# Making twenty gate tiles in pairs with seven half-size products each

## The chip, the cores and the metric

The kernel runs on one core of a Trainium2 chip. The metric is the time of one execution on the device, in microseconds (us). The kernel before takes 2025.02 us (median of three runs, 2023.78 to 2026.5).

Engines are named as the profile names them. PE is the matrix engine: in `matmul(o, w, x)` the second argument is the stationary 128 x 128 operand, the third the moving one, whose columns stream through. PEld is its weight load, which overlaps the matmul. DVE is the vector engine, ACT the scalar (activation) engine, POOL is GpSimd. SP issues DMAs. SBUF is the on-chip working memory and PSUM the memory that matmuls write to, in banks of 512 floats per partition.

## The reference

One layer of a decoder trunk is applied to 2048 prompt positions and to 8 x 8 sample positions. What matters here is the gated merge of three branches:

```python
xn = _rmsnorm(x, p["norm_w"])
h = jnp.einsum("btd,de->bte", xn, p["w_in"])
q, k, v, z_a, gate_b, gate_c, h_b, z_b, u, v_c, z_c, g = _split_cols(h)
...
gates = jax.nn.sigmoid(g + p["b_gate"]).reshape(n, t, N_BRANCHES, D_MODEL)
...
a = jnp.einsum("bte,ed->btd", jax.nn.silu(z_a) * y_a, p["w_out_a"])
b = jnp.einsum("bte,ed->btd", jax.nn.silu(z_b) * y_b, p["w_out_b"])
c = jnp.einsum("bte,ed->btd", jax.nn.silu(z_c) * y_c, p["w_out_c"])
m = gates[:, :, 0] * a + gates[:, :, 1] * b + gates[:, :, 2] * c
return x + jnp.einsum("btd,de->bte", m, p["w_o"])
```

The width is 1024, so `g` has 3072 columns: 24 tiles of 128 columns, each a product of a 1024 x 128 weight with xn. Branches have 512 channels.

## The kernel before

Positions are taken in four blocks (`SBS`): three of 512 positions, and a last one of 576 (512 prompt positions and the 64 sample positions), which is worked in two chunks of 288 columns. Every block goes through the same phases: keys and values, queries, attention (mixed into the next phases), the convolution branch, the chunk branch, the gate phase and the output phase.

All data is float32, and a product is made with two parts of each operand: `split` (L170 and L171) makes the high part by an ACT cast to the format that PE multiplies, and the low part by a DVE subtraction. `gemm_t` then issues three matmuls for each 128 rows of the contraction, high x high, high x low and low x high (L179, L180, L181). The normalised x stands in SBUF as `xh` and `xl`, eight tiles of 128 rows.

Weights come one unit after another in the order that `order()` lists. `load_to` brings a unit by DMA into one of three `raw` tiles (a `wt` unit, that is one gate tile, has 1024 columns, 512 KB), `split_to` splits it into one of four `wh`/`wl` pairs, and `take` hands it to the matmuls. Splits are issued two units ahead of their use, and a load is issued as soon as a raw tile is free. The SP queue works its DMAs in program order, and a DMA that waits for a free tile holds back those behind it. PE and SP follow the program's order. The order of the other engines is set by a scheduler when the program is built; each of these queues is worked in order too.

The gate phase (`gate_phase`) runs over d = 0..7 (128 channels of the model width) and b = 0..2 (the branches). Gate tile j = 3d + b takes 24 matmuls (8 contraction tiles x 3) into one PSUM tile `ps_mm`, of which there are three; ACT applies the sigmoid with its bias (L773) into `t`. Then 12 matmuls make the branch's projection with a `wout` unit (512 columns), DVE multiplies it by the gate (L789) and adds the three branches up (L793). After the third branch the sum is split into `mh` and `ml`, the operands of the output phase. The squares of the next block's x, for its norm, are made in this phase from a tile of their own.

PSUM further holds two `ps_tp` banks for transposes and the banks `S0`, `S1` and `pv`, one tile each, which attention uses; in the gate phase they are idle.

Of the kernel before, what the change touches and what calls it, by code (L numbers as in the profile page):

```python
# [16 lines left out]
P = 128  # L17
# [32 lines left out]
def trunk_kernel(ctx: ExitStack, tc: tile.TileContext, A, O):  # L50
# [9 lines left out]
    def ps_mm():  # L60
        return psum.tile([P, 512], F32, tag="mm", name="ps_mm", bufs=3)
# [36 lines left out]
    def order():  # L98
        for _ in SBS:
            for j in range(6):  # L100
                yield "wn", j
            for j in range(28):
                yield "wt", j
            for j in range(6, 10):
                yield "wn", j
            for j in range(24):
                yield "wt", 28 + j
                yield "wout", j
            for j in range(KT):
                yield "wo", j  # L110

    units = [(n, j, A[n][j]) for n, j in order()]
    loaded, ready, taken = [], [], [0]
    ahead = dict(loads=0, splits=0)

    def load_to(j):
        while len(loaded) < min(j, len(units)):
            src = units[len(loaded)][2]
            raw = raws.tile([P, WE], F32, tag="raw", name="raw")
            nc.sync.dma_start(raw[:, : src.shape[1]], src)  # L120
            loaded.append(raw)

    def split_to(j):
        while len(ready) < min(j, len(units)):
            i = len(ready)
            load_to(i + 1)
            n = units[i][2].shape[1]
            wh = wts.tile([P, WE], F32R, tag="wh", name="wh")
            wl = wts.tile([P, WE], F32R, tag="wl", name="wl")
            split(wh[:, :n], wl[:, :n], loaded[i][:, :n])  # L130
            loaded[i] = None
            ready.append((wh, wl))
            load_to(i + 1 + ahead["loads"])

    def take(name, j):
        i = taken[0]
        assert units[i][:2] == (name, j), (units[i][:2], name, j)
# [58 lines left out]
    def xrstd(sb):  # L196

        t0, _, chunks, _ = SBS[sb]
        n = chunks[-1][1]
        tiles = [(c, min(c + P, n)) for c in range(0, n, P)]  # L200
        st = {"x": res.tile([P, 4 * TMAX], F32, tag="za", name="xbuf")}
        st["r"] = res.tile([P, TMAX], F32, tag="acc", name="acc")[:, :n]
        r = small.tile([P, 8], F32, tag="xr", name="xr")

        def piece(j, c0, c1):
            w = c1 - c0
            x = st["x"][:w, j % 2 * D:(j % 2 + 1) * D]
            nc.sync.dma_start(x, A["xn"][t0 * P + c0:t0 * P + c1])
            nc.scalar.activation(x, x, AF.Square, accum_out=r[:w, j:j + 1])

        def fin():
            for j0, j1, w in ((0, n // P, P), (n // P, len(tiles), n % P)):
                if w and j1 > j0:
                    rstd(r[:w, j0:j1], r[:w, j0:j1], j1 - j0, D)

        def spread():
            for t in (tiles[:4], tiles[4:]):
                if t:
                    ps = ps_tp()
                    b = t[0][0]  # L220
                    for c0, c1 in t:
                        w = c1 - c0
                        nc.tensor.transpose(
                            ps[:, c0 - b:c1 - b], r[:w, c0 // P:c0 // P + 1].broadcast_to([w, P]), ident[:w, :w]
                        )
                    nc.scalar.copy(st["r"][:, b:t[-1][1]], ps[:, : t[-1][1] - b])

        return st, [lambda j=j, c=c: piece(j, *c) for j, c in enumerate(tiles)] + [fin, spread]

    def xsplit(sb, st):  # L230
        t0, _, chunks, _ = SBS[sb]
        n = chunks[-1][1]

        def load(k):
# [12 lines left out]

        return [lambda k=k: piece(k) for k in range(KT)]
# [438 lines left out]
    def chunk_phase(sb, br, samp_args):  # L687
# [12 lines left out]
        br2 = [res.tile([P, 4, TMAX], F32R, tag="br2" + x, name="br2" + x) for x in "hl"]  # L700
        br.append(br2)
        vbuf = res.tile([P, 4 * 1024], F32R, tag="mh", name="vbuf")
        if sample:
            pair_sample("ml")
        def mixed(i, rows, t, gg):

            ts = slice(i * P, i * P + rows)
# [18 lines left out]
        def spatial(i, vh, vl, t, gg):  # L726
# [8 lines left out]
            if gg.stop == 4:  # L735
                mixed(i, P, t, slice(0, 4))

        for i, o, rows in wide(6, wide_outs(ntile, sample)):
            ssq = small.tile([P, 1], F32, tag="vssq", name="vssq")
            vn = tmp("vn", [P, 512])  # L740
            nc.scalar.activation(vn[:rows], o, AF.Square, accum_out=ssq[:rows])
            r = small.tile([P, 1], F32, tag="vr", name="vr")
            rstd(r[:rows], ssq[:rows], 1, 512)
            nc.vector.scalar_tensor_tensor(vn[:rows], o, r[:rows], vnw[:rows], ALU.mult, ALU.mult)
            if i == ntile:
                nc.sync.dma_start(O["scv"], vn[:rows])
                later(AT_SPATIAL + SPATIAL_AFTER * i, lambda vn=vn: spatial_sample(vn))
            else:
                v0 = i * 1024
                vh, vl = vbuf[:, v0:v0 + 512], vbuf[:, v0 + 512:v0 + 1024]  # L750
                split(vh, vl, vn)
                t = side("sp", [P, 4, P])
                for j in range(2):
                    gg = slice(2 * j, 2 * j + 2)
                    later(AT_SPATIAL + SPATIAL_AFTER * i + SPATIAL_EVERY * j, lambda a=(i, vh, vl, t, gg): spatial(*a))

    def keep(new, old):

        tc.keep_in_program_order(nc.scalar.dma_start(O[new][:, : P - TS, :], A[old][:, TS:, :]))

    def gate_phase(sb, br):
        chunks = SBS[sb][2]
        n = chunks[-1][1]
        m = None
        for d in range(KT):
            acc = None
            for b in range(3):
                wg = take("wt", 28 + 3 * d + b)
                t = tmp("t", [P, n])
                for c0, c1 in chunks:  # L770
                    pg = ps_mm()
                    gemm_t(pg, wg, KT, *xr, c0, c1)
                    nc.scalar.activation(t[:, c0:c1], pg[:, : c1 - c0], AF.Sigmoid, bias=bg[:, 8 * b + d:8 * b + d + 1])  # L773
                if d == 0 and b == 2:
                    flush()
                    m = [res.tile([P, KT, TMAX], F32R, tag="m" + x, name="m" + x) for x in "hl"]
                    if sb + 1 < len(SBS):
                        st, xpieces = xrstd(sb + 1)
                        for j, p in enumerate(xpieces):
                            later(2.0 + 4.0 * j, p)  # L780
                    if not sb:
                        later(4.0, lambda: keep("sk", "ck"))
                        later(12.0, lambda: keep("sv", "cvr"))
                wo = take("wout", 3 * d + b)
                brr = (lambda k, x, y, b=b: br[b][0][:, k, x:y], lambda k, x, y, b=b: br[b][1][:, k, x:y])
                for c0, c1 in chunks:
                    pa = ps_mm()
                    gemm_t(pa, wo, 4, *brr, c0, c1)
                    nc.vector.tensor_tensor(t[:, c0:c1], pa[:, : c1 - c0], t[:, c0:c1], ALU.mult)  # L789
                if acc is None:  # L790
                    acc = t
                else:
                    nc.vector.tensor_tensor(acc, acc, t, ALU.add)  # L793
            split(m[0][:, d, :n], m[1][:, d, :n], acc)
# [4 lines left out]
        return m  # L799

    def out_phase(sb, m):
        t0, _, chunks, _ = SBS[sb]
        n = chunks[-1][1]
        mr = (lambda k, a, b: m[0][:, k, a:b], lambda k, a, b: m[1][:, k, a:b])
# [60 lines left out]
    for sb in range(len(SBS)):  # L865
# [13 lines left out]
        chunk_phase(sb, br, (samp, sbuf, za, br))  # L879
        m = gate_phase(sb, br)  # L880
        out_phase(sb, m)


# [122 lines left out]
```

## Time and profile before

| | |
|---|---|
| median of three runs | 2025.02 us |
| the profiled execution's own time | 2026.45 us |
| its span, first to last instruction | 2024.7 us |
| PE busy | 2001.7 us (99%) |
| DVE busy | 1053.7 us (52%) |
| ACT busy | 850.5 us (42%) |
| POOL busy | 79.2 us (4%) |
| gate phase of the first block | from 255.7 us on, 195.3 us |
| gate phase of the last block | begins before 1760 us and ends near 1970 us |

The profile gives, for each engine, how long it was busy, and for each group of equal instructions their count, mean duration and the idle time before them with what ended it. A view of the waits names, for each engine, whom it waited for. The chain of waits is followed back from the last instruction. The timeline lists instructions with their start. A matmul's duration in the records holds its way through the array, so consecutive ones overlap: the distance of their starts is what one costs in a stream.

### The profile page before, as it was taken

The numbers are of one execution on the slowest core, as the hardware profiler recorded it, in microseconds if no ns is written. First come the engines' busy times: TensorE is split into PE (matmuls) and PEld (weight loads), VectorE is DVE, ScalarE is ACT, GpSimd is POOL, SyncE is SP. The second block draws the span as 40 slices with busy tenths as digits, with TensorE's granted clock in tenths as the row PEclk, the third lists the DMA queues.
The fourth block names the chain that finished last, engine by engine and source line by source line (L and its number), as shares of the span: only waits on it lengthen the run. The fifth ranks groups of instructions, "written<-read, shape, count | busy, mean of one in ns | idle before, by whom it ended". The sixth has DMA issues, their size and how long they took to land.

```text
span 2024.7 us, 27228 instructions
## 1 busy us (share of the span) xinstructions
PE 2001.7 (99%) x10811; PEld 1745.5 (86%) x10811; DVE 1053.7 (52%) x1823; ACT 850.5 (42%) x1467; POOL 79.2 (4%) x134
## 2 busy tenths in 40 slices
PE   6999999999999999999999999999999999999999
PEld 5888888888888888888888888888889999999999
DVE  6686263335588353336478635344557852633332
ACT  4675243333476333333267423333347642423220
POOL 2100000000200000000110000000020000000000
PEclk9999999999999999999999999999999999999999
DMA  6222233336322323335422323333622242232333
GB/s 202 89 84 84 84 103 118 121 110 216 99 66 84 94 70 123 115 94 188 147 77 73 94 79 99 126 104 121 214 88 53 55 122 73 66 89 79 84 100 109
DMA packets 85695, 212.25 MB, mean 105 GB/s; under 512 B 18224, under 2 KB 23344, under 8 KB 85552
## 3 DMA queue, kind: packets, MB, share of 16 engines
q1 hardware_dynamic: 85536, 209.53, 34.0%
q8 instruction: 85, 1.39, 0.3%
q10 hardware_dynamic: 32, 0.98, 0.1%
q14 instruction: 42, 0.34, 0.1%
HBM read 201.46 MB, written 10.00 MB: 104 GB/s over the span
## 4 chain that ended last, share of the span: by engine, by line
PE 95%; ACT 2%; DVE 2%; issue 0%; DMA 0%; POOL 0%; SPq 0%; ACTq 0%; DVEq 0%; POOLq 0%
PE ps_mm L180 26%; PE ps_mm L179 26%; PE ps_mm L181 26%; PE ps_mm L300 2%; PE ps_mm L299 2%; PE ps_mm L298 2%; PE wideS L299 1%; PE wideS L298 1%; PE wideS L300 1%; PE ps_tp L520 1%; PE sp L496 1%; PE sp L495 1%; PE pv L528 1%; PE pv L527 1%; PE widepv L300 1%; PE widepv L299 1%
## 5 line engine op out<-in xcount | busy, mean ns | idle before, releaser
L179 PE MATMUL ps_mm<-xh,wh 128*128 128x512 f32 (+1 forms) x2080 | 740.4, 356 | 0.0
L181 PE MATMUL ps_mm<-xh,wl 128*128 128x512 f32 (+1 forms) x2080 | 732.1, 352 | 0.0
L180 PE MATMUL ps_mm<-xl,wh 128*128 128x512 f32 (+1 forms) x2080 | 731.8, 352 | 0.0
L171 DVE TENSOR_TENSOR wl<-raw,wh 128x1024 fp32r<-128x1024 f32 x376 | 407.9, 1085 | 569.5 <-ACT wh L170 567.1
L170 ACT CAST wh<-raw 128x1024 fp32r<-128x1024 f32 x376 | 353.5, 941 | 767.8 <-PE ps_mm L180 550.8
L181 PEld LDWEIGHTS ps_mm<-xh,wl 128*128 128x128 f32 x2080 | 390.3, 188 | 49.5
L180 PEld LDWEIGHTS ps_mm<-xl,wh 128*128 128x128 f32 x2080 | 391.0, 188 | 45.8
L179 PEld LDWEIGHTS ps_mm<-xh,wh 128*128 128x128 f32 x2080 | 390.7, 188 | 45.9
L180 PE MATMUL ps_mm<-ml,wh 128*128 128x512 f32 (+1 forms) x320 | 112.5, 351 | 0.3 <-DVE ml L171 0.3
L181 PE MATMUL ps_mm<-mh,wl 128*128 128x512 f32 (+1 forms) x320 | 112.4, 351 | 0.0
L179 PE MATMUL ps_mm<-mh,wh 128*128 128x512 f32 (+1 forms) x320 | 112.4, 351 | 0.0
L789 DVE TENSOR_TENSOR t<-ps_mm,t 128x512 f32<-128x512 f32 (+1 forms) x120 | 71.6, 597 | 73.9 <-PE ps_mm L181 73.9
L773 ACT ACTIVATE t<-ps_mm,c_bg 128x512 f32<-128x512 f32 (+1 forms) x120 | 73.0, 609 | 69.8 <-PE ps_mm L181 69.7
L298 PE MATMUL ps_mm<-wh,xh 128*128 128x256 f32 (+1 forms) x208 | 71.2, 343 | 5.0 <-ACT xh L170 4.8
L482 ACT ACTIVATE rbuf<-ps_tp,c_qnw 64x256 fp32r<-64x256 f32 x128 | 60.0, 469 | 28.6 <-DVE rbuf L483 20.0
L299 PE MATMUL ps_mm<-wl,xh 128*128 128x256 f32 (+1 forms) x208 | 69.6, 335 | 1.3 <-DVE wl L171 1.3
L300 PE MATMUL ps_mm<-wh,xl 128*128 128x256 f32 (+1 forms) x208 | 70.0, 336 | 0.9 <-DVE xl L171 0.9
L180 PEld LDWEIGHTS ps_mm<-ml,wh 128*128 128x128 f32 x320 | 60.0, 188 | 8.0 <-DVE ml L171 0.6
L179 PEld LDWEIGHTS ps_mm<-mh,wh 128*128 128x128 f32 x320 | 60.0, 188 | 7.5
L181 PEld LDWEIGHTS ps_mm<-mh,wl 128*128 128x128 f32 x320 | 60.0, 188 | 7.5
L506 ACT ACTIVATE sbuf<-sbuf,nm 128x256 f32<-128x256 f32 (+1 forms) x128 | 62.8, 492 | 8.3 <-DVE nm L503 7.9
L812 DVE TENSOR_TENSOR xt<-ps_mm,xt 128x512 f32<-128x512 f32 (+1 forms) x40 | 23.9, 597 | 75.6 <-PE ps_mm L181 44.9
(227 smaller groups left out, 2642.7 us busy)
## 6 DMA issues: line engine op xcount, KB each, us to landing
raw<-in_wt SPq DMA_DIRECT2D x208, 512.0 KB
raw<-in_wout SPq DMA_DIRECT2D x96, 256.0 KB
raw<-in_wn SPq DMA_DIRECT2D x40, 512.0 KB
raw<-in_wo SPq DMA_DIRECT2D x32, 512.0 KB
xbuf<-in_xn SPq DMA_DIRECT2D x12, 512.0 KB
xt<-in_xt SPq DMA_DIRECT2D x24, 256.0 KB
out_yt<-xt SPq DMA_DIRECT2D x24, 256.0 KB
xbuf<-in_xt SPq DMA_DIRECT2D x16, 256.0 KB
```

Source lines behind the costliest of these rows:

```text
L170: nc.scalar.copy(hi, src)
L171: nc.vector.tensor_tensor(lo, src, hi.bitcast(F32), ALU.subtract)
L179: nc.tensor.matmul(o, wh[:, ws], rh(k, c0, c1), start=k == 0, stop=False)
L180: nc.tensor.matmul(o, wh[:, ws], rl(k, c0, c1), start=False, stop=False)
L181: nc.tensor.matmul(o, wl[:, ws], rh(k, c0, c1), start=False, stop=k == kts - 1)
L298: nc.tensor.matmul(o, xh[:, k, ts], wh, start=k == 0, stop=False)
L299: nc.tensor.matmul(o, xh[:, k, ts], wl, start=False, stop=False)
L300: nc.tensor.matmul(o, xl[:, k, ts], wh, start=False, stop=k == KT - 1)
L482: nc.scalar.activation(hh[half, :, e], src, AF.Copy, scale=qnw2[es])
L506: nc.scalar.activation(s[:, h, k0:], s[:, h, k0:], AF.Exp, bias=nm[:, h:h + 1], accum_out=den[:, h:h + 1])
L773: nc.scalar.activation(t[:, c0:c1], pg[:, : c1 - c0], AF.Sigmoid, bias=bg[:, 8 * b + d:8 * b + d + 1])
L789: nc.vector.tensor_tensor(t[:, c0:c1], pa[:, : c1 - c0], t[:, c0:c1], ALU.mult)
```

## The change

Gate tiles 0 to 3 of each block are made as before. The other twenty are taken in pairs, j and j + 1. Their weights, each cut into its first and last 512 contraction rows, form a 2 x 2 block matrix, and x, cut into the same two halves of the contraction (first index) and into two halves of the positions (second index), another. Of their product, which took eight products of quarters, seven are made, by Strassen's scheme in the variant with fewer sums:

- Sums of x (`x_sums`), once per block: t1 = x12 - x11, t2 = x22 - t1, t3 = x22 - x12, t4 = x21 - t2. DVE and ACT make them and their two parts, from `xh` + `xl`. t1 and t2 lie in the tile `ml`, t3 in the tiles of keys and values (`kst`, `vst`), t4 in `za`.
- Sums of weights (`halves`), once per pair, on POOL: s1, the difference of the first halves (which overwrites half of the second raw tile), s2, and the last one, which overwrites s2. Each is an add or subtract of 128 x 512 numbers.
- The units of a pair: four `pair` units of 1024, 1024, 1024 and 512 columns (two, two, two and one half), then `wouts`, both projections in one unit of 1024 columns.
- The seven products (`product`), each 12 matmuls of half the block's columns (256, or 288 in the last block), go to S0, pv, S1, S0, S1, pv, S0 in this order. ACT copies the first out of PSUM, and seven DVE adds of half a tile form the two gate tiles (L949 to L959).
- `merge` then multiplies by the projections and adds up. The sum goes into one float32 tile `m`; its two parts are made only at the end of the phase, seven of eight tiles (`part`) before the last pair's merges.
- The next block's x for the norm is loaded into the three raw tiles instead of a tile of its own, and earlier in the phase.

The core of the diff (line numbers in the orders below are those of the changed kernel):

```diff
+SINGLES = 4
@@ order()
-            for j in range(24):
+            for j in range(SINGLES):
                 yield "wt", 28 + j
                 yield "wout", j
+            for j in range(SINGLES, 24, 2):
+                for i in range(4):
+                    yield "pair", (28 + j, i)
+                yield "wouts", j
@@ load_to
+            src = sources(*units[len(loaded)])
+            if live[0] + len(src) > RAWS and len(loaded) > len(ready):
+                return
...
+    def halves(i, part):
+        add = nc.gpsimd.tensor_tensor
+        if part == 0:
+            r0, r1 = combos["raw"] = loaded[i]
+            s1 = combos["s1"] = side("s1", [P, H])
+            add(s1, r1[:, :H], r1[:, H:], ALU.add)
+            add(r1[:, :H], r0[:, :H], r1[:, :H], ALU.subtract)
+            return r0[:, :H], r1[:, :H]
+        r0, r1 = combos["raw"]
+        if part == 1:
+            s2 = combos["s2"] = side("s2", [P, H])
+            add(s2, combos["s1"], r0[:, :H], ALU.subtract)
+            return s2, combos["s1"]
+        if part == 2:
+            return r0[:, H:], r1[:, H:]
+        add(combos["s2"], r0[:, H:], combos["s2"], ALU.subtract)
+        return (combos["s2"],)
@@ xrstd
-            x = st["x"][:w, j % 2 * D:(j % 2 + 1) * D]
+            x = raws.tile([P, WE], F32, tag="raw", name="xraw")[:w]
@@ x_sums, first(q) for two contraction tiles
+            x11, x12, x22 = whole(q, 1, 1), whole(q, 1, 2), whole(q, 2, 2)
+            nc.vector.tensor_tensor(x11, x12, x11, ALU.subtract)
+            split(t1[0][:, qs], t1[1][:, qs], x11)
+            nc.vector.tensor_tensor(x12, x22, x12, ALU.subtract)
+            split(t3h[:, qs], t3l[q], x12)
+            nc.vector.tensor_tensor(x22, x22, x11, ALU.subtract)
+            split(t2[0][:, qs], t2[1][:, qs], x22)
@@ gate_phase
+        def product(bank, w, half, r):
+            o = psum.tile([P, 512], F32, tag=bank, name="pair" + bank, bufs=1)[:, :h]
+            wh, wl = w
+            rh, rl = sums[r]
+            for k in range(4):
+                ws = slice(half * H + k * P, half * H + (k + 1) * P)
+                nc.tensor.matmul(o, wh[:, ws], rh(k), start=k == 0, stop=False)
+                nc.tensor.matmul(o, wh[:, ws], rl(k), start=False, stop=False)
+                nc.tensor.matmul(o, wl[:, ws], rh(k), start=False, stop=k == 3)
...
+        def pair(j):
+            add = nc.vector.tensor_tensor
+            ta, tb, ca, cb = [tmp(x, [P, n]) for x in ("t", "t", "ca", "cb")]
+            lo, hi = slice(0, h), slice(h, n)
+            p1, u, u3, u5 = ca[:, lo], ca[:, hi], cb[:, lo], cb[:, hi]
+            w = take("pair", (28 + j, 0))
+            nc.scalar.copy(p1, product("S0", w, 0, "11"))
+            p3 = product("pv", w, 1, "t3")
+            w = take("pair", (28 + j, 1))
+            add(u, product("S1", w, 0, "t2"), p1, ALU.add)
+            add(u3, p3, u, ALU.add)
+            p5 = product("S0", w, 1, "t1")
+            add(u5, p5, u, ALU.add)
+            add(tb[:, hi], p5, u3, ALU.add)
+            w = take("pair", (28 + j, 2))
+            add(ta[:, lo], product("S1", w, 0, "21"), p1, ALU.add)
+            add(tb[:, lo], product("pv", w, 1, "t4"), u3, ALU.add)
+            nc.scalar.activation(tb, tb, AF.Sigmoid, bias=bias(j + 1))
+            w = take("pair", (28 + j, 3))
+            add(ta[:, hi], product("S0", w, 0, "22"), u5, ALU.add)
+            nc.scalar.activation(ta, ta, AF.Sigmoid, bias=bias(j))
+            wh, wl = take("wouts", j)
...
+            merge(j, ta, (wh[:, :H], wl[:, :H]))
+            merge(j + 1, tb, (wh[:, H:], wl[:, H:]))
```

The orders of the queues follow, from the first block's gate phase and, for the change, the second block's. DVE before the change, over two gate tiles with their projections: L171 splits a unit, L789 multiplies by the gate, L793 adds a branch.

```order
L789 TENSOR_TENSOR t_2630<-ps_mm_2665,t_2630 128x512
L171 TENSOR_TENSOR wl_2680<-raw_2605,wh_2679 128x1024
L171 TENSOR_TENSOR wl_2713<-raw_2628,wh_2712 128x512
L171 TENSOR_TENSOR wl_2734<-raw_2663,wh_2733 128x1024
L789 TENSOR_TENSOR t_2685<-ps_mm_2718,t_2685 128x512
L171 TENSOR_TENSOR wl_2767<-raw_2683,wh_2766 128x512
L793 TENSOR_TENSOR t_2630<-t_2630,t_2685 128x512
```

DVE of the changed kernel, from the end of one pair's merges to the middle of the next pair. L223 is the split, L897 the multiplication, L903 the branch sum; `wl_7860` is the fourth unit of the coming pair, `wl_7899` its `wouts` unit.

```order
L897 TENSOR_TENSOR t_7649<-ps_mm_7793,t_7649 128x512
L897 TENSOR_TENSOR t_7650<-ps_mm_7807,t_7650 128x512
L223 TENSOR_TENSOR wl_7860<-s2_7784,wh_7859 128x512
L903 TENSOR_TENSOR t_7649<-t_7649,t_7650 128x512
L223 TENSOR_TENSOR wl_7899<-raw_7790,wh_7898 128x1024
L949 TENSOR_TENSOR ca_7824<-pairS1_7868,ca_7824 128x256
L950 TENSOR_TENSOR cb_7825<-pairpv_7846,ca_7824 128x256
L952 TENSOR_TENSOR cb_7825<-pairS0_7883,ca_7824 128x256
L953 TENSOR_TENSOR t_7823<-pairS0_7883,cb_7825 128x256
L223 TENSOR_TENSOR wl_7932<-raw_7864,wh_7931 128x512
```

The split of the `wouts` unit now stands ahead of the add that empties S1 (L949) and of the three adds behind it. With four `wh`/`wl` pairs and five units to a gate pair, that split writes over the weights of the same pair's first unit, which the second product is the last to read.

POOL of the changed kernel, one pair and the beginning of the next: the four sums of weights; before the change nothing stands on POOL in this place.

```order
L154 TENSOR_TENSOR s1_7760<-raw_7693 128x512
L155 TENSOR_TENSOR raw_7693<-raw_7691,raw_7693 128x512
L160 TENSOR_TENSOR s2_7784<-s1_7760,raw_7691 128x512
L164 TENSOR_TENSOR s2_7784<-raw_7691,s2_7784 128x512
L154 TENSOR_TENSOR s1_7933<-raw_7866 128x512
```

The first three are free to start when the pair's two raw tiles have landed, one pair ahead of their use; the fourth waits until DVE has read s2.

More of the change, by code (lines that the diff above doesn't have):

```diff
@@ L126, in split_to @@
             load_to(i + 1)
-            n = units[i][2].shape[1]
+            name, arg = units[i]
             wh = wts.tile([P, WE], F32R, tag="wh", name="wh")
             wl = wts.tile([P, WE], F32R, tag="wl", name="wl")
-            split(wh[:, :n], wl[:, :n], loaded[i][:, :n])
+            if name == "pair":
+                for c, x in enumerate(halves(i, arg[1])):
+                    cs = slice(c * H, (c + 1) * H)
+                    split(wh[:, cs], wl[:, cs], x)
+                live[0] -= 2 if arg[1] == 3 else 0
+            else:
+                n = H if name == "wout" else WE
+                split(wh[:, :n], wl[:, :n], loaded[i][0][:, :n])
+                live[0] -= 1
             loaded[i] = None
@@ L200, in xrstd @@
         tiles = [(c, min(c + P, n)) for c in range(0, n, P)]
-        st = {"x": res.tile([P, 4 * TMAX], F32, tag="za", name="xbuf")}
+        st = {}
         st["r"] = res.tile([P, TMAX], F32, tag="acc", name="acc")[:, :n]
@@ L232, in xsplit @@
         n = chunks[-1][1]
+        st["x"] = res.tile([P, 4 * TMAX], F32, tag="za", name="xbuf")
         def load(k):
@@ L699, in chunk_phase @@
         flush()
-        br2 = [res.tile([P, 4, TMAX], F32R, tag="br2" + x, name="br2" + x) for x in "hl"]
+        br2 = []
         br.append(br2)
@@ L703, in chunk_phase @@
         if sample:
[L704 removed]
+            pair_sample("br2l")
         def mixed(i, rows, t, gg):
@@ L757, in keep, with gate_phase @@
     def keep(new, old):
         tc.keep_in_program_order(nc.scalar.dma_start(O[new][:, : P - TS, :], A[old][:, TS:, :]))
-    def gate_phase(sb, br):
+    def gate_phase(sb, br, xs):
         chunks = SBS[sb][2]
         n = chunks[-1][1]
[L764 to L794, printed above, removed]
@@ new lines, in gate_phase, with bias, merge @@
+        h = n // 2
+        sums, last_sums = xs
+        st = {}
+        if sb + 1 < len(SBS):
+            st, xpieces = xrstd(sb + 1)
+            for j, p in enumerate(xpieces):
+                later(0.5 + 0.75 * j, p)
+        def bias(j):
+            d, b = divmod(j, 3)
+            return bg[:, 8 * b + d:8 * b + d + 1]
+        def merge(j, t, wo):
+            d, b = divmod(j, 3)
+            brr = (lambda k, x, y: br[b][0][:, k, x:y], lambda k, x, y: br[b][1][:, k, x:y])
+            for c0, c1 in chunks:
+                pa = ps_mm()
+                gemm_t(pa, wo, 4, *brr, c0, c1)
+                nc.vector.tensor_tensor(t[:, c0:c1], pa[:, : c1 - c0], t[:, c0:c1], ALU.mult)
+            if b == 0:
+                st["acc"] = t
+            else:
+                acc = st["acc"]
+                out = acc if b == 1 else st["m"][:, d, :n]
+                nc.vector.tensor_tensor(out, acc, t, ALU.add)
@@ new lines, in single @@
+        def single(j):
+            wg = take("wt", 28 + j)
+            t = tmp("t", [P, n])
+            for c0, c1 in chunks:
+                pg = ps_mm()
+                gemm_t(pg, wg, KT, *xr, c0, c1)
+                nc.scalar.activation(t[:, c0:c1], pg[:, : c1 - c0], AF.Sigmoid, bias=bias(j))
+            if j == 2:
+                flush()
+                st["m"] = res.tile([P, KT, TMAX], F32, tag="mh", name="m")
+                for q in range(2):
+                    later(0.25 + 0.75 * q, lambda q=q: last_sums(q))
+                if not sb:
+                    later(4.0, lambda: keep("sk", "ck"))
+                    later(12.0, lambda: keep("sv", "cvr"))
+            merge(j, t, take("wout", j))
@@ new lines, in pair @@
+        def pair(j):
[20 more added lines that the diff above has]
+            wh, wl = take("wouts", j)
+            if j == 22:
+                st["hi"] = res.tile([P, KT, TMAX], F32R, tag="ml", name="mhi")
+                st["lo"] = [res.tile([P, 4, TMAX], F32R, tag="br0" + x, name="mlo" + x) for x in "hl"]
+                for d in range(KT - 1):
+                    part(d)
+            merge(j, ta, (wh[:, :H], wl[:, :H]))
+            merge(j + 1, tb, (wh[:, H:], wl[:, H:]))
@@ L795, in gate_phase, with part @@
+        def part(d):
+            split(st["hi"][:, d, :n], st["lo"][d // 4][:, d % 4, :n], st["m"][:, d, :n])
+        for j in range(SINGLES):
+            single(j)
+        for j in range(SINGLES, 24, 2):
+            pair(j)
+        part(KT - 1)
         flush()
```

83 lines of the change are left out of this document (72 added, 11 removed).

## The prediction

> **What bounds the kernel now.** I read the page's busy times, its PEclk row and its chain of waits first, then the view of the waits for PE, then the gate phases alone, since the change acts there.
>
> ```profile
> PE 2001.7 (99%) x10811; PEld 1745.5 (86%) x10811; DVE 1053.7 (52%) x1823; ACT 850.5 (42%) x1467; POOL 79.2 (4%) x134
> ...
> PEclk9999999999999999999999999999999999999999
> ...
> PE 95%; ACT 2%; DVE 2%; issue 0%; DMA 0%; POOL 0%; SPq 0%; ACTq 0%; DVEq 0%; POOLq 0%
> ```
>
> ```profile
> PE ps_tp L269 <- POOL xr L167: 8.4, 2, 6.6
> ...
> PE ps_mm L180 <- DVE ml L171: 0.3, 1, 0.3
> ```
>
> PE is busy 99%, at full clock, and is 95% of the chain. Its largest wait is 8.4 us in all, outside the gate phase. The windows below lie in the gate phases of the first and the last block; their columns are length, then busy time and count of PE, PEld, DVE, ACT and POOL, the clock, DMA share and GB/s.
>
> ```profile
> 255.70:451.00 195.30, 195.16 (x877) 161.75 (x876) 87.57 (x122) 67.53 (x96) 3.07 (x6) 1.00 0.36 112
> ...
> 1760.00:1970.00 210.00, 210.00 (x1587) 209.93 (x1586) 77.31 (x114) 62.35 (x97) 0.00 (x0) 1.00 0.30 87
> ```
>
> In both PE never rests; DVE works 45% (87.57 of 195.30) and 37%, ACT 35% and 30%, POOL almost nothing. So each matmul taken out gains its slot, as long as DVE, ACT, POOL and the loads keep up.
>
> **What the products save.** A slot is the distance of two starts. First and last row of three stretches of the timeline:
>
> ```profile
> 299.64 0.39 PE L179 MATMUL ps_mm<-br1h,wh 128*128 128x512 f32 x1
> ...
> 301.91 0.39 PE L180 MATMUL ps_mm<-xl,wh 128*128 128x512 f32 x1
> ```
>
> ```profile
> 1799.72 0.29 PE L179 MATMUL ps_mm<-xh,wh 128*128 128x288 f32 x1
> ...
> 1801.97 0.29 PE L181 MATMUL ps_mm<-xh,wl 128*128 128x288 f32 x1
> ```
>
> ```profile
> 500.05 0.28 PE L298 MATMUL ps_mm<-wh,xh 128*128 128x256 f32 x1
> ...
> 508.56 0.29 PE L300 MATMUL ps_mm<-wh,xl 128*128 128x256 f32 x1
> ```
>
> Ten slots of 512 columns take 2.27 us, 0.227 each; 17 of 288 take 2.25, 0.1324 each; 71 of 256 take 8.51, 0.1199 each. Half the columns cost more than half (0.1135), and that eats most of Strassen's eighth: two gate tiles take 48 x 0.227 = 10.90 us, seven products 84 x 0.1199 = 10.07. That is 0.82 us for each of 30 pairs, 24.6 us. In the last block a tile is already worked in chunks of 288, so the width stays and 96 matmuls become 84: 12 x 0.1324 = 1.59 us, ten times, 15.9 us. Together **40.5 us**, the most that the change can give. The 24 matmuls of projection in a pair stay.
>
> **The new chain in a pair.** In a block of 512 the products start at 0, 1.44, 2.88, 4.32, 5.76, 7.20 and 8.63 us; merges fill 10.07 to 15.5. Product 5 writes S1, which DVE's add L949 has to empty. DVE's order has the split of `wouts` ahead of that add, and that split goes into the buffer of the pair's first unit, free only once product 2 has read it. How long these steps take:
>
> ```profile
> 260.72 0.39 PE L180 MATMUL ps_mm<-xl,wh 128*128 128x512 f32 x1
> ...
> 261.19 1.05 ACT L170 CAST wh<-raw 128x1024 fp32r<-128x1024 f32 x1 [1.60 <-PE ps_mm L180]
> ...
> 262.27 1.23 DVE L171 TENSOR_TENSOR wl<-raw,wh 128x1024 fp32r<-128x1024 f32 x1 [1.54 <-ACT wh L170]
> ...
> 263.42 0.42 DVE L733 TENSOR_TENSOR sp<-ps_tp,c_bsb 128x256 f32<-128x256 f32 x1
> ```
>
> ```profile
> 281.28 0.69 DVE L171 TENSOR_TENSOR br2l<-sp,br2h 128x512 fp32r<-128x512 f32 x1 [0.69 <-ACT br2h L170]
> ...
> 282.03 0.50 PE L180 MATMUL ps_mm<-br2l,wh 128*128 128x512 f32 x1
> 282.14 0.19 PEld L181 LDWEIGHTS ps_mm<-br2h,wl 128*128 128x128 f32 x1
> 282.37 0.40 PE L181 MATMUL ps_mm<-br2h,wl 128*128 128x512 f32 x1
> ```
>
> The cast comes 0.08 us after the matmul's end (261.19 - 261.11). The last high-part reader in product 2 is matmul 23, started at 22 x 0.1199 = 2.64 and over 0.28 later: the cast starts at 3.00 and ends at 4.05, DVE's split starts at 4.08 (0.03 later, as above), the next DVE operation 1.15 after it (263.42 - 262.27), at 5.23, and L949 with 256 columns from PSUM ends at 5.65. PE follows 0.06 later (282.03 - 281.97), at 5.71, and product 5 is due at 5.76. The slack is about **0.06 us**; in the last block, with slots of 0.1324, the same steps give 0.34. Before, this chain was not there: three `ps_mm` banks rotated.
>
> An interrupted PE also restarts slowly: 0.34 between the two starts above where 0.227 is the slot, 0.11 more for each wait.
>
> **What may be late on it: POOL.** DVE itself has room. A pair's work on it is four splits of 1024 columns, one of 512, seven adds of half a tile and the four operations of the merges: 4 x 1.22 + 0.68 + 7 x 0.42 + 4 x 0.69 = 11.3 us of 15.5. ACT has four casts of 1024 (1.05 each), one of 512, a copy and two sigmoids, some 6.7 us. The groups of 301 to 451 us (busy us, mean ns, then idle before):
>
> ```profile
> L171 DVE TENSOR_TENSOR wl<-raw,wh 128x1024 fp32r<-128x1024 f32 x19 | 23.2, 1223 | 56.9 <-ACT wh L170 56.9
> ...
> L789 DVE TENSOR_TENSOR t<-ps_mm,t 128x512 f32<-128x512 f32 x19 | 13.1, 691 | 24.7 <-PE ps_mm L181 24.7
> L171 DVE TENSOR_TENSOR wl<-raw,wh 128x512 fp32r<-128x512 f32 x18 | 12.3, 683 | 7.1 <-ACT wh L170 7.1
> ...
> L773 ACT ACTIVATE t<-ps_mm,c_bg 128x512 f32<-128x512 f32 x18 | 12.3, 683 | 25.4 <-PE ps_mm L181 25.4
> ...
> L793 DVE TENSOR_TENSOR t<-t 128x512 f32<-128x512 f32 x13 | 8.9, 686 | 0.1
> ...
> L209 ACT ACTIVATE xbuf<-xbuf 128x1024 f32<-128x1024 f32 x3 | 3.2, 1059 | 3.2 <-DMA xbuf<-in_xn 3.2
> ```
>
> But POOL's four adds of 512 columns per pair are new, and POOL and DVE meet:
>
> ```profile
> 513.67 1.22 DVE L171 TENSOR_TENSOR wl<-raw,wh 128x1024 fp32r<-128x1024 f32 x1
> ...
> 513.85 1.10 POOL L166 TENSOR_SCALAR kr<-ks 128x2 f32<-128x2 f32 x1 [3.25 <-DVE ks L344]
> ```
>
> ```profile
> L166 POOL TENSOR_SCALAR xr<-xr 128x4 f32<-128x4 f32 x1 | 0.2, 199 | 107.2 <-ACT xbuf L209 107.2
> ```
>
> ```profile
> 54.29 1.23 DVE L171 TENSOR_TENSOR wl<-raw,wh 128x1024 fp32r<-128x1024 f32 x1 [4.22 <-ACT wh L170]
> 54.56 1.46 POOL L852 TENSOR_SCALAR_AFFINE_SELECT wsr<-wsr 128x512 f32<-128x512 f32 x1 [16.94 <-DMA wsr<-in_wst]
> ...
> 56.48 1.64 POOL L167 TENSOR_TENSOR qr<-qr,mhalf 128x8 f32<-128x8 f32 x1
> 56.70 0.69 DVE L171 TENSOR_TENSOR wsp<-wsr,wsp 128x512 fp32r<-128x512 f32 x1 [0.59 <-ACT wsp L170]
> ```
>
> A POOL operation that takes 0.20 took 1.10 beside a DVE split and ended with it (514.95 against 514.89): POOL was held. That DVE is held by POOL no row shows: the split at 56.70 kept its 0.69 us, but that POOL operation reads eight columns. An add on POOL is priced from L852: it ended 0.50 after DVE did (56.02 against 55.52), with one input of 512 columns; two inputs make about 1.0 as an estimate, with 0.5 and 1.46 as bounds.
>
> [...]
>
> POOL's first three adds are free to run once the raw tiles have landed, early in the cycle, with each DVE split in between; by my count the second ends and the third begins near 4.1, where the `wouts` split wants to start. Delay of that split: nothing at the seam, 1.0 in the worst case of one add; I take a third, 0.33, because the meeting is near the seam. Then a pair loses 0.33 - 0.06 + 0.11 = 0.38, times 30 = 11.4 us; in the last block the 0.34 covers most, 0.15 x 10 = 1.5.
>
> **Moved work that I cost at little.** `x_sums`, some 26 DVE operations a block and as many of ACT, goes into the chunk phase and the first four tiles, where by the windows both engines have over half their time free. Without that cover it would be 26 x 0.62 = 16 us a block. The parts of the sum `m` come as a burst before the last pair's merges; only the last part stands between the merges and the output phase. Its cast and subtraction stood there before too, for each eighth tile, and cost PE 0.3 us (the second row of the waits); I take 0.3 more for each block, 1.2 in all, since a whole add now goes ahead of them.
>
> As many bytes of weights are loaded as before. The next block's x for the norm now passes through the three raw tiles, on SP's queue among the weights, and each holds a tile for its load and for ACT's reading (L209 above, 1.06 us). The one load with a row of its own is the program's first:
>
> ```profile
> 2.17 5.30 DMA raw<-in_wn
> ```
>
> A pair takes three raw tiles per 15.5 us, one in 5.2, so even at 5.30 the ring about keeps pace. A pair whose weights stand behind a load of x could wait for one load, 5 us, in three blocks (15 us): that is the upper end. I take the lower, nothing, because the DMA engines are busy only 0.36 of the first window, so loads in flight don't slow each other much, and the order of loads has the x tiles spread over the phase.
>
> **The sum.** 2026.45 (the profiled execution) - 40.5 + 12.9 + 1.2 = 2000.0; it stands 1.4 above the median of the runs shown, so **1999 us**. Own range 1992 to 2010.
>
> **Rivals.**
> - *POOL doesn't hold DVE up*, as at 56.70: without the 12.9, 1986 us. For it: no row shows DVE held. Against it: the row at 513.85 shows one shared resource. 0.33.
> - *Each pair waits for a whole add*, 1.0: (1.0 - 0.06 + 0.11) x 30 + (1.0 - 0.34 + 0.11) x 10 = 39.2, up to 2025 us. 0.10, spread from 2010 to 2025.
> - *The x loads in the raw ring* delay a pair's weights by 5 us in three blocks, the upper end above: 2014 us. For it: three tiles serve both. Against it: the DMA share of 0.36. 0.05.
> - *It doesn't do what it says*: 256 columns next to half-filled banks run at 0.13 in place of 0.1199 (84 x 0.01 x 30 = 25 us): 2025 us. The 71 even slots speak against it. 0.03.
> [...]
>
> **How the numbers follow.** The forecast has 0.42. A measurement can tell 0.2%, 4 us. Faster, below 2021: 0.42 + 0.33 + 0.05 + 0.06 of the whole-add case = 0.86; same 0.04 + 0.03 = 0.07; slower 0.07. From 1982 (4 us below the free case) to 2020 lie about 0.85.
>
> **What would show it.** Products of 256 columns at 0.12 a slot, and 84 of them per pair; on PE, waits of L949's add before product 5, 0.2 to 0.5 us each; POOL adds near 1 us, longer beside splits; DVE splits of 1024 columns above 1.23 where POOL works. No such waits mean 1986. Waits of over 1 us per pair, waits for raw tiles in a first pair, or DVE late in the chunk phase would make it wrong.

## The result and the profile after

The changed kernel takes 2015.22 us, the kernel before 2025.33 us in the same comparison: a ratio of 0.9948, 95% interval 0.9937 to 0.9958. That is 10 us faster, where 26 were forecast. The sign is right, but the time lies 5 us above the upper end of the range that was given (1992 to 2010), and the gain is less than half of the one forecast. The two profiled executions, by which the ledger below goes, took 2026.45 and 2013.36 us, 13.1 us apart.

The page of the changed kernel: span, busy times, and the chain.

```profile
span 2011.6 us, 30272 instructions
...
PE 1972.3 (98%) x11771; PEld 1765.4 (88%) x11771; DVE 1365.2 (68%) x2367; ACT 945.1 (47%) x1679; POOL 335.0 (17%) x294
...
PE 89%; DVE 5%; ACT 4%; DMA 1%; issue 1%; POOL 1%; SPq 0%; ACTq 0%; DVEq 0%; POOLq 0%
```

DVE went from 1054 to 1365 us and POOL from 79 to 335, and 11% of the chain is now not PE's, where it was 5%. The view of PE's waits names the places (us in total, times, longest; idle time alone, without what restarting costs):

```profile
...
PE pairS L929 <- DVE ca L949: 7.9, 18, 1.3
PE ps_tp L275 <- POOL xr L219: 7.7, 1, 7.7
...
PE ps_mm L231 <- ACT mhi L222: 0.9, 1, 0.9
...
PE ps_mm L232 <- DVE mlol L223: 0.4, 1, 0.4
```

Neither of the first two rows shown was there before. The first is the wait forecast: product 5 for the add that empties S1. The second was not: PE stood 7.7 us, once, for the norm of the next block's x. The products themselves run as forecast, here the first and last of eleven matmuls of 256 columns in a row, 1.20 us for ten slots:

```profile
311.84 0.28 PE L929 MATMUL pairS<-xsum,wh 128*128 128x256 f32 x1
...
313.04 0.28 PE L930 MATMUL pairS<-xl,wh 128*128 128x256 f32 x1
```

A ledger follows from all matmuls of both traces. From each distance to the next start the slot for its width is taken away (0.227, 0.1326, 0.1200 us), and what is left is summed by place. Us, against the kernel before:

| | forecast | trace |
|---|---|---|
| fewer or narrower slots | -40.5 | -40.5 |
| product 5, blocks of 512 | +11.4 | +11.0 |
| product 5, last block | +1.5 | +3.7 |
| last part of m | +1.2 | +1.3 |
| norm of the next x | 0 | +10.9 |
| all else | 0 | +0.5 |
| sum | -26.4 | -13.1 |

So the two traces differ from the forecast by 13.3 us, and 10.9 of these lie at the one place that the forecast had at nothing.

**Product 5** in one pair. DVE, POOL and PE each in their own timeline, with DVE's idle time in brackets:

```profile
406.28 2.33 DVE L223 TENSOR_TENSOR wl<-raw,wh 128x1024 fp32r<-128x1024 f32 x1 [1.99 <-ACT wh L222]
408.54 0.41 DVE L949 TENSOR_TENSOR ca<-pairS,ca 128x256 f32<-128x256 f32 x1
408.98 0.42 DVE L950 TENSOR_TENSOR cb<-pairpv,ca 128x256 f32<-128x256 f32 x1
```

```profile
404.86 1.30 POOL L154 TENSOR_TENSOR s<-raw 128x512 f32<-128x512 f32 x1 [5.47 <-DMA raw<-in_wt]
406.24 1.29 POOL L155 TENSOR_TENSOR raw<-raw 128x512 f32<-128x512 f32 x1
407.49 2.27 POOL L160 TENSOR_TENSOR s<-s,raw 128x512 f32<-128x512 f32 x1
```

```profile
407.83 0.28 PE L931 MATMUL pairS<-xsum,wl 128*128 128x256 f32 x1
409.00 0.38 PE L929 MATMUL pairS<-xh,wh 128*128 128x256 f32 x1 [0.89 <-DVE ca L949]
409.22 0.28 PE L930 MATMUL pairS<-xl,wh 128*128 128x256 f32 x1
```

The split of `wouts` began 0.04 us after POOL's second add had begun, and took 2.33 us in place of 1.23, 1.10 more; POOL's third add, which met the split in turn, took 2.27 in place of about 1.28. Product 5 was due at 407.95 and began at 409.00, with a first slot of 0.22. Over the whole kernel:

```profile
L223 DVE TENSOR_TENSOR wl<-raw,wh 128x1024 fp32r<-128x1024 f32 x240 | 306.5, 1277 | 229.6 <-ACT wh L222 227.8
L223 DVE TENSOR_TENSOR wl<-raw,wh 128x512 fp32r<-128x512 f32 x176 | 155.2, 901 | 42.5 <-ACT wh L222 41.3
```

Splits of 512 columns take 901 ns in the mean, where they took 683. So POOL does hold DVE. The 11.0 us of the blocks of 512 aren't all made at this one split, though: it took longer than alone in 16 of the 30 pairs, by 0.26 us in the mean over all 30. Three other pairs lost 0.65, 1.6 and 0.35 us because DVE came late to the split or to the add; in the two larger, an operation further ahead in its queue had been held (a split of x sums at 291.74 with 1.62 us, a branch sum at 356.53 with 1.78, both in place of some 0.69).

In the last block the split is held longer, by 0.57 us in the mean, in nine of ten pairs. Held by 0.15 us, as in the first two rows below, a pair loses nothing; held by 1.13, as in the last two, it loses 0.86:

```profile
1852.34 1.37 DVE L223 TENSOR_TENSOR wl<-raw,wh 128x1024 fp32r<-128x1024 f32 x1 [2.24 <-ACT wh L222]
1853.63 0.44 DVE L949 TENSOR_TENSOR ca<-pairS,ca 128x288 f32<-128x288 f32 x1
...
1923.29 2.35 DVE L223 TENSOR_TENSOR wl<-raw,wh 128x1024 fp32r<-128x1024 f32 x1 [1.14 <-ACT wh L222]
1925.56 0.44 DVE L949 TENSOR_TENSOR ca<-pairS,ca 128x288 f32<-128x288 f32 x1
```

**The norm of x**, in the third block's gate phase: SP, then ACT, then POOL, then PE.

```profile
1221.59 3.05 SPq L140 DMA_DIRECT2D raw<-in_wt  x2
1224.84 0.98 SPq L260 DMA_DIRECT2D xraw<-in_xn  x1
```

```profile
1232.11 0.62 ACT L222 CAST wh<-raw 128x512 fp32r<-128x512 f32 x1 [2.76 <-POOL raw L155]
1232.63 1.05 ACT L261 ACTIVATE xraw<-xraw 64x1024 f32<-64x1024 f32 x1
```

```profile
1229.44 1.29 POOL L154 TENSOR_TENSOR s<-raw 128x512 f32<-128x512 f32 x1 [3.47 <-DMA raw<-in_wt]
1230.81 1.26 POOL L155 TENSOR_TENSOR raw<-raw 128x512 f32<-128x512 f32 x1
...
1233.86 0.63 POOL L218 TENSOR_SCALAR xr<-xr 64x1 f32<-64x1 f32 x1 [0.56 <-ACT xraw L261]
1234.58 0.87 POOL L219 TENSOR_TENSOR xr<-xr,mhalf 64x1 f32<-64x1 f32 x1
```

```profile
1227.23 0.60 PE L275 MATMUL ps_tp<-c_ident,xr 128*128 128x128 f32 x4
1235.50 0.36 PE L275 MATMUL ps_tp<-c_ident,xr 64*128 64x64 f32 x1 [7.67 <-POOL xr L219]
1235.80 0.79 PE L231 MATMUL ps_mm<-br2h,wh 128*128 128x512 f32 x1
1236.39 0.63 PE L232 MATMUL ps_mm<-br2l,wh 128*128 128x512 f32 x1
1236.81 0.63 PE L233 MATMUL ps_mm<-br2h,wl 128*128 128x512 f32 x1
```

This phase prepares the last block, whose 576 rows need a fifth piece of x. Its load was issued at 1224.84, behind two tiles of weights. ACT's reading of it stands behind the cast of the first pair's weights, which waits for POOL's sums, which wait for the weights to land at 1229.44. The DMA engines moved 12 GB/s from 1229 to 1230 and nothing from 1230 to 1231, so x was there by 1230; the 2.6 us from then until ACT read it are its place in ACT's queue. The power on POOL comes after that, and PE's order has the transpose of the result ahead of the third tile's projection. So PE rested from 1227.8 to 1235.5. Afterwards the slots are 0.427 us (1236.81 to 1237.24 and on) in place of 0.227 until 1241.8: the wait costs 7.8, the slow slots behind it 3.1.

### The profile page after: what moved, and what is told of

Same layout as the page of the kernel before. It is cut to its first block, busy times and chain, and to the rows that moved or that the text cites. A ratio compares the mean times of both kernels' runs of the same rounds, so it can differ in the third digit from the quotient of the medians.

```text
span 2011.6 us, 30272 instructions
## 1 busy us (share of the span) xinstructions
PE 1972.3 (98%) x11771; PEld 1765.4 (88%) x11771; DVE 1365.2 (68%) x2367; ACT 945.1 (47%) x1679; POOL 335.0 (17%) x294
## 4 chain that ended last, share of the span: by engine, by line
PE 89%; DVE 5%; ACT 4%; DMA 1%; issue 1%; POOL 1%; SPq 0%; ACTq 0%; DVEq 0%; POOLq 0%
PE ps_mm L231 18%; PE ps_mm L232 18%; PE ps_mm L233 18%; PE pairS L929 4%; PE pairS L930 4%; PE pairS L931 4%; DVE wl L223 3%; PE pairpv L930 2%; PE pairpv L929 2%; PE pairpv L931 2%; PE ps_mm L353 2%; PE ps_mm L352 2%; PE ps_mm L351 2%; ACT wh L222 2%; PE wideS L353 1%; PE wideS L352 1%
## 5 line engine op out<-in xcount | busy, mean ns | idle before, releaser
L223 DVE TENSOR_TENSOR wl<-raw,wh 128x1024 fp32r<-128x1024 f32 (+1 forms) x416 | 461.7, 1118 | 272.1 <-ACT wh L222 269.1
L222 ACT CAST wh<-raw 128x1024 fp32r<-128x1024 f32 (+1 forms) x416 | 354.7, 866 | 539.1 <-PE ps_mm L232 232.7
L231 PE MATMUL ps_mm<-xh,wh 128*128 128x512 f32 (+1 forms) x1280 | 460.2, 360 | 0.0
L233 PE MATMUL ps_mm<-xh,wl 128*128 128x512 f32 (+1 forms) x1280 | 451.7, 353 | 0.0
L232 PE MATMUL ps_mm<-xl,wh 128*128 128x512 f32 (+1 forms) x1280 | 451.6, 353 | 0.0
L233 PEld LDWEIGHTS ps_mm<-xh,wl 128*128 128x128 f32 x1280 | 241.0, 188 | 30.7
L232 PEld LDWEIGHTS ps_mm<-xl,wh 128*128 128x128 f32 x1280 | 241.5, 189 | 27.1
L231 PEld LDWEIGHTS ps_mm<-xh,wh 128*128 128x128 f32 x1280 | 241.3, 189 | 27.3
L929 PE MATMUL pairS<-xh,wh 128*128 128x256 f32 (+1 forms) x480 | 140.1, 292 | 8.1 <-DVE ca L949 7.9
L897 DVE TENSOR_TENSOR t<-ps_mm,t 128x512 f32<-128x512 f32 (+1 forms) x120 | 70.8, 593 | 58.5 <-PE ps_mm L233 57.3
L929 PE MATMUL pairS<-xsum,wh 128*128 128x256 f32 (+1 forms) x320 | 91.7, 287 | 0.0
L930 PE MATMUL pairS<-xsum,wh 128*128 128x256 f32 (+1 forms) x320 | 91.6, 286 | 0.0
```

The lines of the kernel that those rows point to most:

```text
L222: nc.scalar.copy(hi, src)
L223: nc.vector.tensor_tensor(lo, src, hi.bitcast(F32), ALU.subtract)
L231: nc.tensor.matmul(o, wh[:, ws], rh(k, c0, c1), start=k == 0, stop=False)
L232: nc.tensor.matmul(o, wh[:, ws], rl(k, c0, c1), start=False, stop=False)
L233: nc.tensor.matmul(o, wl[:, ws], rh(k, c0, c1), start=False, stop=k == kts - 1)
L929: nc.tensor.matmul(o, wh[:, ws], rh(k), start=k == 0, stop=False)
```

## Experiments

Five questions were asked: what the norm of x costs and where; why product 5 waits; whether the losses add; which blocks gain; and what is left.

### The norm of x

Two edits take away the wait, each in its own way. The first, x out of the raw tiles and later:

```diff
-            x = raws.tile([P, WE], F32, tag="raw", name="xraw")[:w]
+            m = st["m"].rearrange("p k t -> p (k t)")
+            x = m[:w, 4 * TMAX + j % 2 * D:4 * TMAX + (j % 2 + 1) * D]
...
-            for j, p in enumerate(xpieces):
-                later(0.5 + 0.75 * j, p)
@@ single(j), behind flush() and the tile m
+                if sb + 1 < len(SBS):
+                    for i, p in enumerate(xpieces):
+                        later(2.0 + 2.5 * i, p)
```

> The next block's x for the norm no longer passes through the raw tiles: it lies in the unused last half of the sum m, and its pieces are spread behind the third gate tile. Theory: the fifth piece of x (there is one only for the last block) stood behind weights in the ring of raw tiles and made PE wait 7.7 us at 1235 us, and the lower clock after that wait cost 2.6 us more; both go, so about 10 us less than the changed kernel, 2005 us, and product 5 keeps its waits (14 us in all). Rival: the wait is one of load bandwidth, or some other load is then late in its place: 2011 to 2015 us, with a wait of several us elsewhere.

Measured: 2004.61 us, ratio to the kernel before 0.9897 (0.9883 to 0.9912). No wait for the norm is left in the gate phase; product 5 keeps 13.4 us by the ledger, and three new waits for `br2h`, 2.5 us in all, have come.

The second leaves x where it is, and moves only the last two steps:

```diff
-            for j, p in enumerate(xpieces):
+            for j, p in enumerate(xpieces[:-2]):
                 later(0.5 + 0.75 * j, p)
@@ single(j), behind flush() and the tile m
+                if sb + 1 < len(SBS):
+                    for i, p in enumerate(xpieces[-2:]):
+                        later(3.0 + 0.75 * i, p)
```

> x still passes through the raw tiles at the same places, but the norm's last steps (the power on POOL, then PE's transposes) are asked for some 16 us later in the program, behind the third gate tile. Theory: the fifth load of x is late by the ring, and what makes it cost time is that PE's order has the transposes in front of the third tile's projection: the wait of 7.7 us and the slow clock behind it go, 2005 us. Rival: the load in the ring itself costs, since the first pair's weights are then late by as much: a wait of 5 us or more elsewhere in the third block, 2010 us or more.

Measured: 2007.56 us, 0.9912 (0.9897 to 0.9927). The wait for the norm is gone and no wait for weights has taken its place, so the late load cost its time through the place of the transposes in PE's order alone. Of the 10.9 us some came back at product 5, which now loses 18.9 by the ledger in place of 14.7.

The third asks whether this part does it alone, in the kernel before:

```diff
-            x = st["x"][:w, j % 2 * D:(j % 2 + 1) * D]
+            x = raws.tile([P, WE], F32, tag="raw", name="xraw")[:w]
@@ gate_phase, at its beginning and no longer behind flush()
+        if sb + 1 < len(SBS):
+            st, xpieces = xrstd(sb + 1)
+            for j, p in enumerate(xpieces):
+                later(0.5 + 0.75 * j, p)
```

> The kernel before with this part of the change alone: the next block's x loaded into the three raw tiles, from the beginning of the gate phase on. Theory: the ring and the early place cost by themselves, 8 to 11 us in the third block, where x has a fifth piece: 2034 us. Rival: only the pairs, which take two raw tiles at once, make the fifth load late: within 2 us of the kernel before.

Measured: 2035.33 us, 1.0048 (1.0031 to 1.0065), slower by 10 us without any pair in it. PE's waits there:

```profile
PE ps_tp L223 <- POOL xr L167: 8.3, 4, 3.8
```

The amount is that of the theory, the place only half: by the ledger 2.0 and 1.9 us fall into the first two blocks, 5.0 into the third, with 2.3 of slow slots behind it. So the ring and the early place cost by themselves; the pairs' sums on POOL are not needed for it, though they add to it where they stand ahead of x. This run has the ring and the early place together; the early place with a tile of its own for x was not run.

### Product 5

Three edits. POOL writes constants and reads nothing:

```diff
-            add(s1, r1[:, :H], r1[:, H:], ALU.add)
-            add(r1[:, :H], r0[:, :H], r1[:, :H], ALU.subtract)
+            nc.gpsimd.memset(s1, 0.5)
+            nc.gpsimd.memset(r1[:, :H], 0.5)
@@ and in the same way for the two sums into s2
```

> The four sums of weights of a pair are replaced by constants that POOL writes without reading SBUF (so the gate tiles are not the reference's); all dependencies stay. Theory: POOL's reading adds hold DVE's splits (0.68 becomes 1.3 to 1.7, 1.23 becomes 2.3), and that is what makes product 5 wait: splits at 0.68 and 1.23 throughout, waits of product 5 from 14 to under 2 us, about 2002 us. Rival: DVE is simply late by its own load and by the order of its queue (slack 0.06 us): the waits stay above 9 us and the time within 4 us of 2015.

Measured: 1998.17 us, 0.9865 (0.9850 to 0.9880).

```profile
L223 DVE TENSOR_TENSOR wl<-raw,wh 128x1024 fp32r<-128x1024 f32 x240 | 293.1, 1221 | 250.9 <-ACT wh L222 249.3
L223 DVE TENSOR_TENSOR wl<-raw,wh 128x512 fp32r<-128x512 f32 x176 | 117.2, 685 | 31.9 <-ACT wh L222 30.5
```

The splits are back at 1221 and 685 ns, and product 5 loses 1.3 us in all. But a constant also takes less than half of an add's time on POOL (0.52 us), so this run alone doesn't part the holding of DVE from a shorter chain. The next one does: the same sums, read and written at the same places, on DVE.

```diff
-        add = nc.gpsimd.tensor_tensor
+        add = nc.vector.tensor_tensor
```

> The four sums of weights of each pair on DVE in place of POOL. If the holding of the ports is all that makes product 5 late, and DVE has room (11.3 us of work in 15.5), the waits go: 2002 to 2006 us. Rival: four more operations of 0.68 us in DVE's queue, one of them ahead of the split of wouts, cost as much as the holding did: 2013 us or more, with waits of product 5 as before.

Measured: 2001.81 us, 0.9887 (0.9872 to 0.9901); product 5 loses 5.6 us. The runs show how long operations of DVE and POOL take with and without each other; the ports that the expectation names they don't show. DVE has 160 more operations:

```profile
PE 1966.4 (98%) x11771; PEld 1762.6 (88%) x11771; DVE 1392.4 (70%) x2527; ACT 944.1 (47%) x1679; POOL 80.6 (4%) x134
```

Their 160 x 0.68 = 109 us raise its busy time by only 27 (from 1365.2), since its time held by POOL is gone. Beside POOL's constants, without these operations, it was busy 1299.8 us, so some 65 of the 1365 us had been held time. And this run shows how near the chain was counted. In a pair in which DVE is not behind, product 4 ends with the matmul at 327.31, and product 5 comes a slot later:

```profile
325.75 1.22 DVE L223 TENSOR_TENSOR wl<-raw,wh 128x1024 fp32r<-128x1024 f32 x1 [1.36 <-ACT wh L222]
326.90 0.42 DVE L949 TENSOR_TENSOR ca<-pairS,ca 128x256 f32<-128x256 f32 x1
```

```profile
327.31 0.28 PE L931 MATMUL pairS<-xsum,wl 128*128 128x256 f32 x1
327.43 0.32 PE L929 MATMUL pairS<-xh,wh 128*128 128x256 f32 x1
327.59 0.28 PE L930 MATMUL pairS<-xl,wh 128*128 128x256 f32 x1
```

L949 ends at 327.32 and product 5 begins at 327.43, with a first slot of 0.16 in place of 0.12. The chain arrives within 0.04 us of its due time, where the forecast had a slack of 0.06. Of the 30 pairs in the blocks of 512, 25 lose no more than this; the other five lose 0.7 to 1.1 us.

The third edit frees PE from the chain:

```diff
-            o = psum.tile([P, 512], F32, tag=bank, name="pair" + bank, bufs=1)[:, :h]
+            o = ps_mm() if bank == "mm" else psum.tile([P, 512], F32, tag=bank, name="pair" + bank, bufs=1)
+            o = o[:, :h]
...
-            p5 = product("S0", w, 1, "t1")
+            p5 = product("mm", w, 1, "t1")
@@ and "mm" in place of S1 and pv for the fifth and sixth product
```

> Products 4, 5 and 6 go to the three ps_mm banks in place of S0, S1 and pv, so product 5 has not to wait until DVE has emptied S1. Theory: the wait is on the bank alone, and nothing else is late: 13 us less than the changed kernel, about 2002 us. Rival: DVE is behind as a whole, and PE waits next for a split of weights or for a ps_mm bank at the merges: less than half is gained, 2009 us or more.

Measured: 1998.70 us, 0.9869 (0.9852 to 0.9885). Product 5 loses nothing; the splits stay long (1292 and 914 ns). DVE is still held by POOL, and it no longer costs time, since nothing that PE waits for hangs on it.

### Whether the losses add

The first edit of x and the edit of the banks, both as shown above, in one kernel:

> Both edits: x in the last half of m, products 4 to 6 in the ps_mm banks. If the two losses are separate they add: 2015 - 10 - 13 = 1992 us, and a gate phase without waits above 0.5 us. If one of them only hides the other, or a new wait takes their place: 2000 us or more.

Measured: 1991.44 us, 0.9834 (0.9819 to 0.9848). The two losses are separate and nearly add. Waits above 0.5 us are left, against the expectation: the three for `br2h` (1.5 us each by the ledger) and one for the last part of m in the last block.

### Which blocks gain

```diff
+        for block in SBS:
+            singles = 24 if block[3] else SINGLES
...
-            for j in range(SINGLES):
+            for j in range(singles):
```

> The changed kernel with the last block's 24 gate tiles made singly; the first three blocks keep their pairs. Theory by slots: the last block's pairs save 16.0 us and lose 3.7 in waits of product 5, so without them the kernel takes 12 us more, 2024 to 2028 us, about as long as before: the three blocks of 512, which should have given 24.6, lose nearly all of it to waits (11 us at product 5, 10 us at the norm of x). Rival: the blocks of 512 carry the gain: 2018 us or less.

Measured: 2026.07 us, 1.0004 (0.9994 to 1.0013). The three blocks of 512 give nothing in the changed kernel: of their 24.6 us, product 5 takes 10.8 and the norm of x 11.1 by this run's ledger, and the 2.7 left are gone in small losses that were not parted. The whole gain of the change, 10.9 us by 2026.07 - 2015.22, comes from the last block.

### What is left

Three kernels put the edits shown above together, without new ones: the late norm with the other banks, the same with the sums on DVE, and the late norm with the sums on DVE in the old banks.

> The norm's last steps behind the third gate tile, and products 4 to 6 in the ps_mm banks; x stays in the raw tiles. If the ledger of the waits is whole, this leaves only the 14.4 + 4.5 us of product 5 out of the run with the late norm: 2007.6 - 18.9 = 1988.7 us. If the ring of raw tiles still costs something that the waits of product 5 had covered, pairs wait for their weights and the time is 1995 us or more.

> As the run before, and the sums of weights on DVE in place of POOL. Once no product waits for DVE, it should not matter who makes the sums: within 2 us of 1988.7. If POOL's holding still delays something else on PE's path, 2 to 5 us faster; if DVE's four extra operations a pair do, slower.

> The norm's last steps behind the third gate tile, and the sums of weights on DVE, with the banks as in the changed kernel. By the run with the sums on DVE, which lost 5.6 us at product 5 and 8.3 at the norm of x: 2001.8 - 8.3 = 1993.5 us, some 4 us behind the run with other banks. Rival: the late norm shifts DVE's work onto product 5 as it did with POOL's sums (18.9 in place of 14.7): 1997 us or more.

Measured: 1989.43 us, 0.9821 (0.9806 to 0.9836); 1988.29 us, 0.9816 (0.9802 to 0.9831); 1996.68 us, 0.9854 (0.9838 to 0.9871). The first two agree with the ledger, and with each other: once no product waits for DVE, it doesn't matter who makes the sums. The third came out beside its rival (1997 or more) and not at 1993.5. Product 5 loses 7.8 us there, against 5.6 without the late norm, as it rose from 14.7 to 18.9 with the sums on POOL. The difference lies in the first two pairs of the third block, which lose 1.46 and 1.39 us, against 0.70 and 0.04 without the late norm. In the second of them DVE's first three sums of weights stand ahead of the `wouts` split, as they do without the late norm, but here they had to wait for their weights:

```profile
1259.18 0.69 DVE L154 TENSOR_TENSOR s<-raw 128x512 f32<-128x512 f32 x1 [1.42 <-DMA raw<-in_wt]
...
1261.12 1.22 DVE L223 TENSOR_TENSOR wl<-raw,wh 128x1024 fp32r<-128x1024 f32 x1
```

The split was due at 1259.76, by the 4.08 us that it stands behind the pair's first matmul elsewhere. Why these weights came later stays open.

The second of these is 37 us faster than the kernel before and 27 faster than the change. It comes within 4 us of the 2025.5 - 40.5 = 1985.0 that the matmul slots alone would give. The largest wait that its gate phases leave is the one at the last part of m:

```profile
PE ps_mm L231 <- ACT mhi L222: 0.9, 1, 0.9
```

## Why the prediction was right or wrong

**Slots: right.** 0.1199 and 0.1324 us a slot were forecast, 0.1200 and 0.1326 came, and so 40.5 us and not an eighth of the gate phase; the rival of slower slots of 256 columns is out.

**The new chain and its slack: right.** The place (product 5 for L949, behind the split of `wouts`), the slack of 0.06 (even to 0.04 where DVE is not held) and the price of a restart (0.10 more for the first slot, against 0.11) came out as worked.

**POOL holds DVE: right, and the rival in which it doesn't is out.** That a split waits for an add of POOL under way, on which the 12.9 us of the sum rest, no row of the kernel before shows; it was the author's assumption. The runs showed it: splits of 512 columns took 901 ns in the mean in the changed kernel, and 685 with POOL's constants in place of its adds. The estimate of 1.0 us for POOL's add was low; alone it takes 1.26 to 1.30. The third of an add per pair that was taken, with slack and restart 0.38 us, came out as 0.37 in the blocks of 512 (11.0 over 30). That the average is so near is partly luck: single pairs lose between nothing and 1.6 us, and the split itself is held by 0.26 us in the mean, less than the 0.33 taken, while the rest of the loss has other places. In the last block the term was mis-sized, 3.7 in place of 1.5. The larger slack of 0.34 was there, but the split is held by 0.57 us in the mean, where the sum took the same 0.33 as for the other blocks. What POOL's operation does mattered: splits of 1024 columns took up to 2.35 us beside POOL's adds, and 1221 ns in the mean with POOL's constants, which only write. DVE's adds from PSUM, with one input from SBUF, were not held: L949 took 0.41 to 0.45 us in the 25 of 40 cases in which an add of POOL ran beside it, and the same in the other 15.

**Slower than before (0.07): out.** 2015 us came, and no split of `wouts` is held by more than 1.13 us, which is less than one add of POOL.

**Two smaller readings.** The last part of m came to 1.3 us where 1.2 were taken, but the forecast had 0.3 in each block, and the wait (the two rows with `mhi` and `mlol` above) stands once, in the last block: the sum is near by luck. And the working counted four splits of 1024 columns and one of 512 for a pair; the kernel makes one of 1024 and seven of 512. By the same durations that is 11.7 us of DVE's time in place of 11.3, which changes nothing in the forecast.

**The failed step** is "I take the lower, nothing", for the next block's x in the raw tiles. It was 10.9 us of the 13.3 that the traces miss, and 10.6 and 7.7 us in the two runs that mend it. The forecast looked at the ring of tiles for a late weight of a pair, and priced that as a rival (5 us in three blocks, 2014 us). That rival had the right edit and nearly the time that was measured, but not the mechanism: no pair waited for its weights. The late thing was the other party of the ring, x itself, first in the order of loads and then in ACT's queue. The same edit also moved the norm forward from behind the third tile to the beginning of the phase, and the `flush()` behind the third tile then sets its transposes in PE's order at a fixed place, ready or not. That half of the edit was told in the change ("earlier in the phase") and was given no price. Nor was the fifth piece seen, which only the last block has. Of the 16 us between forecast and median, 10.9 are this, 2.2 are product 5 in the last block, and 3.0 are that the profiled executions lie 13.1 apart where the medians lie 10.1.

## What to carry to other kernels

When an edit moves a step forward in the program, ask of each engine that takes part where its queue now has that step, and what must have landed by then; an earlier place in an in-order queue is a due time (here it cost PE a wait of 7.7 us). A tile pool that two streams share can delay either of them (here x, and no weights of a pair), so both have to be priced. A wait between engines with a slack of less than one instruction (here 0.06 us) is paid for when a third engine interferes (here 11.0 us over 30 pairs); a free bank was the better repair here, at 1998.70 us against 2001.81 with the sums on DVE.

## What the runs showed of the hardware

After PE had waited 5.9 us or more for the norm of x, its next slots of 512 columns took 0.427 us in place of 0.227 (the slots from 1236.81 on, above), and the granted clock was 0.50 (from 1236.5 to 1241.0). The waits with this were 5.9, 6.6, 7.8, 8.7 and 8.8 us, in five kernels (the sums on DVE, POOL's constants, the change itself, the other banks, the last block made singly); in a sixth (x in the ring of the kernel before) it was one of 4.0 us that followed a wait of 1.0 with only four transposes between. The extra time was 1.7 to 3.1 us each, with no order by the length of the wait. In the changed kernel PE stopped at 1227.8, the clock stood at 1.00 until 1231.5 and at 0.50 from there to 1241.7, 10.2 us; 6.2 us of these lie behind the wait, and the extra time is half of them. Waits of 1.9 and 2.0 us at the same place, in the sixth kernel, were followed by normal slots. Each of the six waits thus cost its length and 1.7 to 3.1 us more.

POOL and DVE delay each other. In the changed kernel POOL's add of 512 columns with two inputs took 1.26 to 1.30 us alone and up to 2.31 beside a split, DVE's split of 1024 columns at most 1.23 without an add beside it and up to 2.35 with one.
